# A hybrid encoder layer on one core: two small tiles shift the right-hand pools, and the recurrence's squares are emitted later

## The chip, the cores and the metric

The kernel runs on one core of a Trainium2 chip. The metric is the device time of one execution in microseconds (us), the median of several runs. TensorE multiplies (PE in the rows, PEld for its weight loads), VectorE is DVE, ScalarE is ACT, GpSimd is POOL, and SyncE (SP) issues the DMAs.

## The reference

One layer over a sequence of 1024 positions, width 1024, all in float32:

```
proj = rms_norm(x) @ w_in                       # 512 LRU + 512 gate + 256 + 128 + 32 columns
xc   = depthwise_conv(lru_x)                    # 4 taps
for each direction:                             # forward and backward
    r, i = sigmoid(xc @ w_a + b_a), sigmoid(xc @ w_x + b_x)      # 8 blocks of 64 x 64
    a    = exp(-8 * r * softplus(-lambda))
    h    = scan(a, sqrt(1 - a^2) * (i * xc))    # h_t = a_t h_(t-1) + u_t
y_lru = gelu(lru_g) * (h_forward + h_backward)
y_mla = attention(8 heads, 96 wide keys, 64 wide values)
h = x + concat(rms_norm(y_lru), rms_norm(y_mla)) @ w_o
u = depthwise_conv(rms_norm(h) @ w_up)          # 1024 -> 2 * 2816, 3 taps
out = rms_norm(h + (silu(u[:2816]) * u[2816:]) @ w_down)
```

The group norm of `y_lru` needs, for each position, the sum of the squares of its 512 channels.

## The kernel before, in words

Every product of two float32 matrices is made of three products of a coarse part and a remainder (`split`, lines 60 to 67, and `mm3`, lines 69 to 72), so a 128x128 weight block is loaded for each 128x512 matmul.

**The recurrence.** The 512 channels are four tiles `j` of 128 partitions by 1024 positions. A tile passes through projection (`proj_x`, `proj_g`), convolution (`conv_a`: one ACT instruction, three on DVE; `conv_b`: the split), four gates (`gate`: PE, then a tanh on ACT), decay (`decay_exp`, `square_a`, `decay_tanh` on ACT, `decay_mul` on DVE), a square root on ACT that needs another activation table (`root`), `gated` and `scale_in` (direction 0 on DVE, direction 1 on POOL), the scans on DVE (`scan`), `add_dirs`, two gelu steps and `merge`, which writes `y_lru[:, j]`. `squares(j, t1)` (lines 239 to 247) squares that tile on ACT; for `j` = 0 it writes the sum `qs`, for the others it overwrites the gelu's tile `t1`, and POOL adds that to `qs`. `qs` is read only in the middle of the attention, by `pss` (line 858).

**Who sets the order.** Tiles 0 and 1 stand in the loop over `j`, in a block where only PE keeps the order of the program. The planner of the compiler puts the other engines' instructions in an order of its own: on its own timeline an engine takes the instruction, among those whose inputs are there, that was emitted first. So an instruction can run ahead of many that are emitted before it. After the loop, from `xc3 = conv_a(3)`, a block begins in which PE, ACT, DVE and POOL all keep the order of the program; tiles 2 and 3 lie in it. There `root()` of tile 2 is followed by `gated` and `scale_in` for both directions, `load_kv` (ACT writes the coarse part of `wkv`, POOL its remainder), `scan(0)`, the first gelu step, `scan(1)`, `add_dirs`, and the gates of tile 3. PSUM has three "big" buffers; the projection `psG2` takes the one that the first gate of tile 2 gives back.

**The memory.** SBUF pools are stacked from the left (`cst`, `sm`, `xtp`, `stp`, `wp`, later `ap`, `fw`) and from the right (`keep`, `ctpool`, `xp`, `lp2`, `lp`, `ap2`, `op`, `fp`). A right-hand pool lies below the one opened before it, and its first tile lies lowest. By the kernel's memory map the left-hand matrix tiles begin at multiples of 128 bytes in a partition. The right end is at byte 229,344, which is 32 over a multiple of 64, and since the right-hand matrix tiles are multiples of 512 bytes long, they all begin 32 over a multiple of 64 (96 over a multiple of 128). On the right lie `cT` (latents, and later three of the output projection's weights), `xch` and `gwt` (gate operands), `wn` (latent projection weights), `kt1` (the keys of odd heads), `yl`, `wo67` in `keep`, and `T1`, `T3`, `T4` in `fp`.

**The up projection.** The FFN's first product is done in 22 pairs of column blocks. Each pair is seven products of 12 matmuls (`PRODUCTS`, `prod`, lines 1067 to 1075), in the order 1, 5, 6, 2, 7, 3, 4. The streamed operand of a product is one of seven 512-column forms: `B11`, `B21`, `B22` and `T2` lie on the left (`xtp`), `T1`, `T3` and `T4` on the right (`fp`). The loaded operand `W` is on the left from pair 2 on; for pairs 0 and 1 the first one is a part of `wo345`, on the right.

Of the kernel before, what the change touches and what calls it, by code (L numbers as in the profile page):

```python
# [10 lines left out]
F32 = mybir.dt.float32  # L11
# [6 lines left out]
P = 128  # L18
D = 1024
S = 1024  # L20
NT = S // P
# [9 lines left out]
CH = 2  # L31
NCHUNK = NPAIR // CH
EPS = 1e-6
GK = math.sqrt(2.0 / math.pi)

V_CW, V_CB, V_GB, V_LAM, V_GO, V_FW, V_FB = 0, 16, 20, 36, 44, 52, 184
# [4 lines left out]
def encoder_layer(ctx, tc, x, w_in, wq, wk, wv, gw, wo, wup, wdn, vec, g_mix, g_ffn, g_fin, g_q, g_kv, tab_t, tab_n, out):  # L41
# [6 lines left out]
    def sbpool(name, bufs=1, side="left"):  # L48
        return tc.tile_pool(name=name, bufs=bufs, side=side, reuse_waits="tile")
# [28 lines left out]

    def rsqrt_dve(sq, ss, n, scale, name, bias=-0.5 * EPS):
        def s1(tag):  # L80
            return sm.tile([P, n], F32, tag="%s%d" % (tag, n), bufs=4 if n == 1 else 1, name=name + tag)
        xh, r0, t, t2, r = s1("xh"), s1("r0"), s1("t"), s1("u"), s1("r")
        dve.tensor_scalar(out=xh, in0=ss, scalar1=-0.5 * scale, scalar2=bias, op0=ALU.mult, op1=ALU.add)
        dve.reciprocal(r0, sq)
        dve.tensor_mul(t, r0, r0)
        dve.tensor_mul(t2, t, xh)
        dve.scalar_tensor_tensor(out=r, in0=t2, scalar=1.5, in1=r0, op0=ALU.add, op1=ALU.mult)
        return r
# [37 lines left out]
    eps_c = cst.tile([P, 1], F32, name="eps_c")  # L126
    pool.memset(eps_c, EPS)
    ones = cst.tile([P, 1], F32, name="ones")
# [7 lines left out]

    right = ExitStack()
    keep = right.enter_context(sbpool("keep", side="right"))
    ctp = ExitStack()
    ctpool = ctp.enter_context(sbpool("ctpool", side="right"))  # L140
    cT = ctpool.tile([P, 2, 3, S], F32R, tag="cT", name="cT")
# [73 lines left out]
    def root():  # L215
        act.activation(bc[:, 0:2, :], bc[:, 0:2, :], AF.Sqrt, scale=-0.0625)
# [18 lines left out]
    def gelu_b(t1, p):  # L235
        act.activation(t1, t1, AF.Tanh, scale=GK)
        dve.scalar_tensor_tensor(out=t1, in0=t1, scalar=1.0, in1=p, op0=ALU.add, op1=ALU.mult)

    def squares(j, t1, eng="act"):
        if j == 0:  # L240
            act.activation(qs, y_lru[:, j, :], AF.Square)
            return
        if eng == "act":
            act.activation(t1, y_lru[:, j, :], AF.Square)
        else:
            pool.tensor_tensor(out=t1, in0=y_lru[:, j, :], in1=y_lru[:, j, :], op=ALU.mult)
        pool.tensor_tensor(out=qs, in0=qs, in1=t1, op=ALU.add)
# [4 lines left out]
    if True:  # L252
        with sbpool("xp", side="right") as xp:
# [37 lines left out]
                xT.append([xtp.tile([P, NK, 512], F32R, tag="xT", name=f"xT{hf}{z}") for z in range(2)])  # L291
            lat = keep.tile([P, NT, NAT], F32, tag="keepB", name="lat")
            kp_nat = keep.tile([P, S], F32R, tag="kpT", name="kpT")
            ss_x = xp.tile([P, NT], F32, name="ss_x")
            ss_l = xp.tile([P, NT, 2], F32, name="ss_l")

            def square(i):
# [162 lines left out]
        if True:  # L460
            def conv_a(j):
                p = psx[j]
                xc = lp.tile([P, S], F32, tag=f"xc{j % 2}", name=f"xc{j}")
                cw = lambda t: vv[:, V_CW + 4 * j + t:V_CW + 4 * j + t + 1]
                act.activation(xc, p, AF.Identity, scale=cw(2), bias=vv[:, V_CB + j:V_CB + j + 1])
                dve.scalar_tensor_tensor(out=xc[:, 2:], in0=p[:, :-2], scalar=cw(0), in1=xc[:, 2:], op0=ALU.mult, op1=ALU.add)
                dve.scalar_tensor_tensor(out=xc[:, 1:], in0=p[:, :-1], scalar=cw(1), in1=xc[:, 1:], op0=ALU.mult, op1=ALU.add)
                dve.scalar_tensor_tensor(out=xc[:, :-1], in0=p[:, 1:], scalar=cw(3), in1=xc[:, :-1], op0=ALU.mult, op1=ALU.add)
                return xc

            def conv_b(j, xc):
                xch = lp.tile([P, 2, S], F32R, tag="xch", name=f"xch{j}")
                split(xch[:, 0], xch[:, 1], xc, "dve", "dve")
                return xc, xch

            def conv(j):
                return conv_b(j, conv_a(j))

            def gate(j, d, g):
                gwt, xch = got[f"g{j}"], cv[j][1]  # L480
                psg = bigA(f"psg{j}{d}{g}")
                b = 2 * d + g
                for hf in range(2):
                    mm3(psg[:, ts(hf, 512)], (gwt[:, 0, b, :], gwt[:, 1, b, :]),
                        (xch[:, 0, ts(hf, 512)], xch[:, 1, ts(hf, 512)]), True, True)
                act.activation(bc[:, 2 * g + d, :], psg, AF.Tanh, scale=0.5, bias=gb_h[:, 4 * j + b:4 * j + b + 1])

            def gated(j, d):
                dve.scalar_tensor_tensor(out=bc[:, 2 + d, :], in0=bc[:, 2 + d, :], scalar=1.0, in1=cv[j][0], op0=ALU.add, op1=ALU.mult)

            def a_tiles(j):
                return [lp2.tile([P, S], F32, tag="a", bufs=2, name=f"a{j}{d}") for d in range(2)]

            def a2_tile(j, d):
                return lp.tile([P, S], F32, tag="a2", name=f"a2{j}{d}")

            def t1_tile(j):
                return (lp2 if j % 2 else lp).tile([P, S], F32, tag="gt", name=f"t1{j}")

            def load_gates(j, gst=None):  # L500
                if gst is None:
                    gst = stp.tile([P, 4, P], F32, tag="st", name=f"gst{j}")
                    nc.sync.dma_start(out=gst, in_=gw[:, j])
                g = lp.tile([P, 2, 4, P], F32R, tag="gw", name=f"gwt{j}")
                split(g[:, 0], g[:, 1], gst, "act", "pool")
                return g

            got = {"X1": wx1, "G0": wG0, "g0": load_gates(0, gst0)}

            def load(k, j):  # L510
                got[f"{k}{j}"] = load_gates(j) if k == "g" else load_w((0 if k == "X" else 512) + j * P, f"w{k}{j}", w_in, "act")

            cv = {0: conv(0)}
            proj_x(1, got["X1"])
            cv[1] = conv(1)
            order.close()
            order.enter_context(tc.manual_schedule(engines=ORDER_PE))
            for j in range(2):
                load("X", j + 2)
                aa = a_tiles(j)  # L520
                gate(j, 0, 0)
                gate(j, 1, 0)
                for d in range(2):
                    a2 = a2_tile(j, d)
                    decay_exp(j, d, aa[d])
                    square_a(aa[d], a2)
                    decay_tanh(j, d)
                    decay_mul(d, a2)
                proj_g(j, got[f"G{j}"], 0)
                gate(j, 0, 1)  # L530
                gate(j, 1, 1)
                root()
                for d in range(2):
                    gated(j, d)
                    scale_in(d)
                    scan(d, aa[d])
                add_dirs(dve)
                proj_g(j, got[f"G{j}"], 1)
                t1 = t1_tile(j)
                gelu_a(t1, psG[j])  # L540
                gelu_b(t1, psG[j])
                load("g", j + 1)
                load("G", j + 1)
                proj_x(j + 2, got[f"X{j + 2}"])
                if j == 0:
                    cv[2] = conv(2)
                merge(j, t1, dve)
                squares(j, t1)
            load("G", 3)


# [21 lines left out]
    proj_g(2, got["G2"], 1)  # L573
    decay_mul(1, a2)
    root()
    gated(2, 0)
    gated(2, 1)
    scale_in(0)
# [3 lines left out]
    t1 = t1_tile(2)  # L582
# [522 lines left out]
    fp = fpx.enter_context(sbpool("fp", side="right"))  # L1105
    for f in ("T1", "T3", "T4"):
        B[f] = fp.tile([P, 2, 4, 512], F32R, name=f)
    C11 = {1: fp.tile([P, S], F32, tag="c", bufs=4, name="s1c")[:, lo]}
    for j in range(3):
        tr_sum("T1", j, spare)  # L1110
    copy(C11[1], S1)
    add(C11[1], VL[1], C11[1])
    prod(6, 0, VL[0], False)
# [156 lines left out]
    def norm3_half(i):  # L1270
        junk = fw.tile([P, 512], F32, tag="w3", bufs=2, name=f"jg{i}")
        act.activation(junk, hh[i][:, hi], AF.Square, accum_out=ss_f[:, i:i + 1])
        for k, m in ((0, 1.0), (1, -0.5)):
            dve.tensor_scalar(out=part[:, k, i:i + 1], in0=ss_f[:, i:i + 1], scalar1=m / D, scalar2=m * EPS, op0=ALU.mult, op1=ALU.add)

# [5 lines left out]
    def norm3_dve(i, sq, part_only=False):  # L1281
        r = rsqrt_dve(sq, ss_f[:, i:i + 1], 1, 1.0 / D, f"rf{i}", part[:, 1, i:i + 1] if part_only else -0.5 * EPS)
        for c in ((lo, hi) if i == NT - 1 else (slice(0, D),)):
# [46 lines left out]
    for j in range(1, NPAIR):  # L1330
# [13 lines left out]
        if j > 1:  # L1344
            GL = bank("GL", f"gl{j}")
            C11[j] = GL
            copy(GL, vl)
# [12 lines left out]
        if j > 1:  # L1360
            prod(2, j, C11[j], False)
        VH[e] = bank(f"H{e}", f"vh{j}")
# [7 lines left out]
        else:  # L1370
# [5 lines left out]
            make(3)  # L1376
        cgs[j] = conv_start(j, C11[j])
        prod(3, j, GH, False)
        add(GH, GH, ts_)
        if not last:  # L1380
            prod(4, j, vl, False)
            glu_gate(j, C11[j], GH)
            fetch_raw(j + 2, 1)
# [142 lines left out]
```

## Time and profile before

| what | value |
|---|---|
| median of 3 runs | 1216.63 us (1215.02 to 1218.22) |
| the profiled execution's own time | 1217.72 us |
| its span, first to last instruction | 1215.9 us (1.8 us lie around it) |
| granted TensorE clock, mean | 0.99 of full speed |
| busy share of the span | PE 96%, PEld 80%, DVE 76%, ACT 54%, POOL 20% |
| chain that ended last, by engine | PE 82%, DVE 10%, ACT 3%, DMA 2%, issue 2% |

The chain that ended last is followed back from the last instruction, at each step to what released it. Where it is all PE, only PE's pace counts; where it changes engines, a delay of any link counts. The stages by the trace: norm and latents to 78 us, the recurrence to about 200 us (it overlaps the attention's first tiles), attention to 440 us, output projection and the FFN's first pair to about 615 us, the other pairs of the up projection to about 1005 us, the down projection to the end.

### The profile page before, as it was taken

To read this page: it belongs to the slowest core of one execution; us is meant where nothing else is said; L and a number is where in the kernel's file an instruction comes from. 1 tells how busy PE (TensorE), PEld (TensorE's weight loads), DVE (VectorE), ACT (ScalarE), POOL (GpSimd) and SP (SyncE) were. 2 spreads that over 40 slices of the span, in tenths; PEclk is the share of its full clock that TensorE was granted. 3 is DMA by queue.
4 is the path that set the end of the run, shared out by engine and by line. 5 is a ranking of instruction groups with operands and counts; after the bars stand their busy time and mean duration, and the time that the engine had idled before them with its cause. 6 is when DMAs were issued, how large, how long until landed. Compare 5 with 4: busy or idle time off the path is not lost.

```text
span 1215.9 us, 15339 instructions
## 1 busy us (share of the span) xinstructions
PE 1165.4 (96%) x5668; PEld 970.0 (80%) x5668; DVE 925.7 (76%) x1371; ACT 656.4 (54%) x1055; POOL 241.9 (20%) x138
## 2 busy tenths in 40 slices
PE   5999997999999999998999999999999999999997
PEld 5977775788889888776778888888888888888885
DVE  6787879777777755587687877877787876887866
ACT  5736687776777763343554454444454454443453
POOL 2213435621212433352011110101011000000000
PEclk9999989999999999998999999999999999999999
DMA  5311101000000142230243223332323259753233
GB/s 214 98 42 44 44 18 35 18 1 1 1 1 1 53 157 87 73 118 18 61 130 122 96 78 111 106 113 81 110 95 121 87 173 334 262 183 112 96 113 121
DMA packets 93579, 113.38 MB, mean 93 GB/s; under 512 B 5184, under 2 KB 59840, under 8 KB 93504
## 3 DMA queue, kind: packets, MB, share of 16 engines
q1 hardware_dynamic: 93504, 112.40, 27.9%
q8 instruction: 44, 0.72, 0.3%
q14 instruction: 31, 0.25, 0.1%
HBM read 82.76 MB, written 28.57 MB: 92 GB/s over the span
## 4 chain that ended last, share of the span: by engine, by line
PE 82%; DVE 10%; ACT 3%; DMA 2%; issue 2%; SPq 0%; DVEq 0%; POOL 0%; ACTq 0%
PE vl L1075 19%; PE x L1268 9%; PE y L1268 7%; PE gh L1075 5%; PE gl L1075 4%; PE pt L762 4%; PE p L1075 4%; PE av L773 3%; PE av L772 3%; PE sc L70 2%; PE sc L71 2%; PE sc L72 2%; DVE bc L223 2%; PE pso L71 1%; PE pso L72 1%
## 5 line engine op out<-in xcount | busy, mean ns | idle before, releaser
L1075 PE MATMUL vl<-T,w 128*128 128x512 f32 x792 | 195.7, 396 | 1.8 <-ACT gl L1081 1.5
L1075 PEld LDWEIGHTS vl<-T,w 128*128 128x128 f32 x792 | 148.6, 188 | 37.6 <-ACT gl L1081 1.9
L67 POOL TENSOR_TENSOR w<-rg,w 128x1024 fp32r<-128x1024 f32 x21 | 52.0, 2474 | 363.6 <-ACT w L62 212.3
L62 ACT ACTIVATE ptb<-pt 128x512 fp32r<-128x512 f32 x128 | 70.1, 596 | 57.5 <-PE pt L762 56.3
L748 DVE TENSOR_REDUCE nm<-sc 128x1 f32<-128x1024 f32 x64 | 78.2, 1222 | 29.9 <-PE sc L72 29.6
L67 DVE TENSOR_TENSOR ptb<-pt,ptb 128x512 fp32r<-128x512 f32 x128 | 83.1, 681 | 7.0 <-ACT ptb L62 7.0
L755 ACT ACTIVATE pr<-sc,nm 128x1024 f32<-128x1024 f32 x64 | 71.7, 1121 | 4.2 <-DVE nm L748 4.1
L762 PE MATMUL pt<-ident,pr 128*128 128x128 f32 x512 | 67.7, 274 | 3.8 <-DVE ptb L67 3.8
L762 PEld LDWEIGHTS pt<-ident,pr 128*128 128x128 f32 x512 | 59.2, 140 | 14.7 <-DVE ptb L67 6.0
L1075 PE MATMUL gh<-B,w 128*128 128x512 f32 x264 | 64.4, 393 | 1.4 <-DVE T L67 1.4
L1172 ACT ACTIVATE c<-gh,vv 128x512 f32<-128x512 f32 x22 | 17.1, 778 | 89.1 <-DVE gh L1078 89.1
L772 PE MATMUL av<-ptb,vt 128*128 128x256 f32 x256 | 64.9, 292 | 0.0
L773 PE MATMUL av<-ptb,vt 128*128 128x256 f32 x256 | 62.6, 283 | 0.0
L1075 PE MATMUL p<-T,w 128*128 128x512 f32 x252 | 62.5, 397 | 0.0
L1268 PE MATMUL x<-abS 128*128 128x512 f32 x264 | 60.2, 389 | 0.0
L1268 PE MATMUL y<-abS 128*128 128x512 f32 x264 | 60.2, 389 | 0.0
L1075 PEld LDWEIGHTS gh<-B,w 128*128 128x128 f32 x264 | 49.5, 188 | 13.0 <-DVE T L67 1.6
L1075 PE MATMUL vl<-B,w 128*128 128x512 f32 x240 | 58.4, 392 | 0.0
L1268 PEld LDWEIGHTS x<-abS 128*128 128x128 f32 x264 | 49.6, 188 | 10.3
L1268 PEld LDWEIGHTS y<-abS 128*128 128x128 f32 x264 | 49.6, 188 | 10.3
L1075 PE MATMUL gl<-B,w 128*128 128x512 f32 x240 | 57.7, 389 | 0.0
L1075 PEld LDWEIGHTS p<-T,w 128*128 128x128 f32 x252 | 47.4, 188 | 11.4
(646 smaller groups left out, 2953.8 us busy)
## 6 DMA issues: line engine op xcount, KB each, us to landing
rg<-in_wup SPq DMA_DIRECT2D x22, 512.0 KB, 3.9
rv<-in_wup SPq DMA_DIRECT2D x22, 512.0 KB, 3.7
S<-c SPq DMA_DIRECT2D x44, 256.0 KB, 2.6
wr<-in_wdn SPq DMA_DIRECT2D x44, 256.0 KB, 5.4
stS<-S SPq DMA_DIRECT2D x44, 256.0 KB, 2.9
A<-c SPq DMA_DIRECT2D x33, 256.0 KB, 2.1
stA<-A SPq DMA_DIRECT2D x33, 256.0 KB, 4.0
wost<-in_wo SPq DMA_DIRECT2D x8, 512.0 KB, 3.7
```

The lines of the kernel that those rows point to most:

```text
L62: act.activation(hi, src, AF.Copy)
L67: (dve if lo_on == "dve" else pool).tensor_tensor(out=lo, in0=src, in1=hi.bitcast(F32), op=ALU.subtract)
L70: pe.matmul(ps, l[0], r[0], start=start, stop=False)
L71: pe.matmul(ps, l[0], r[1], start=False, stop=False)
L72: pe.matmul(ps, l[1], r[0], start=False, stop=stop)
L748: dve.reduce_max(nm[t], sc[t], axis=AX, negate=True)
L755: act.activation(pr[t], sc[t], AF.Exp, bias=nm[t], accum_out=rowsum[:, h, i:i + 1])
L762: pe.transpose(pt[:, ts(c, P)], pr[t][:, ts(4 * kh + c, P)], ident)
L772: pe.matmul(av[:, 0:256], lv, ptb[buf][:, 0, c, :], start=(c == 0), stop=False)
L773: pe.matmul(av[:, 0:256], lv, ptb[buf][:, 1, c, :], start=False, stop=(c == NT - 1))
L1075: pe.matmul(ps, w[:, l, ko + k, :], b[:, r, k, :], start=a_, stop=z_, skip_group_check=True)
L1268: pe.matmul(ps, ab[:, 0, l, ts(j, P)], ab[:, 1, r, :], start=a_, stop=z_, skip_group_check=True)
```

## The change

`ss_x` (32 bytes per partition) is allocated first in `keep` instead of in `xp`. So `ctpool` and every right-hand pool opened above it on the stack (`xp`, `lp2`, `lp`, `ap2`, `op`) moves 32 bytes down, while the other tiles of `keep` stay. In `xp` the tiles behind the old place of `ss_x` move with it. In `fp` a tile of 24 floats (96 bytes) that nothing reads is put behind `T1`, `T3` and `T4`, which moves these three 96 bytes down; the `c` tiles behind it stay. And `squares(0)` is emitted behind the `root()` of tile 1 in the loop, `squares(1, t1)` behind the `root()` of tile 2, which is in the block where all engines keep the program's order. No arithmetic changes.

```diff
+PAD = 24
...
     keep = right.enter_context(sbpool("keep", side="right"))
+    ss_x = keep.tile([P, NT], F32, name="ss_x")
     ctp = ExitStack()
...
-            ss_x = xp.tile([P, NT], F32, name="ss_x")
...
                 gate(j, 0, 1)
                 gate(j, 1, 1)
                 root()
+                if j == 1:
+                    squares(0, None)
                 for d in range(2):
...
                 merge(j, t1, dve)
-                squares(j, t1)
             load("G", 3)
...
     decay_mul(1, a2)
     root()
+    squares(1, t1)
     gated(2, 0)
     gated(2, 1)
     scale_in(0)
...
     for f in ("T1", "T3", "T4"):
         B[f] = fp.tile([P, 2, 4, 512], F32R, name=f)
+    fp.tile([P, PAD], F32, name="pad")
```

## Rows read from the trace of the kernel before

**Rows 1.** By stretch: us; busy PE, PEld, DVE, ACT, POOL (count); PE clock, DMA, GB/s
```profile
230.00:330.00 100.00, 99.66 (x651) 88.62 (x652) 77.53 (x123) 70.29 (x135) 24.73 (x18) 1.00 0.00 1
...
600.00:1005.00 405.00, 403.49 (x1744) 327.42 (x1743) 322.05 (x423) 195.29 (x260) 46.23 (x19) 1.00 0.33 108
```

**Rows 2.** Chain that ended last, one pair: start us, us on the chain, what
```profile
617.73 2.72 PE gl L1075 x12
620.45 2.81 PE vl L1075 x12
623.26 2.76 PE gh L1075 x12
626.02 5.57 PE vl L1075 x24
...
637.17 2.72 PE gl L1075 x12
```

**Rows 3.** Instructions of the PSUM tile gl: duration ns min/median/max, first and last start
```profile
L1075 PE MATMUL gl<-B,w x240: 388/389/390, 617.6 to 989.4; 128*128 128x512 f32 x120
L1075 PE MATMUL gl<-B,wo x12: 392/397/478, 554.9 to 557.5; 128*128 128x512 f32 x12
```

**Rows 4.** Busy time of the score matmuls (sc) alone, heads 2 and 3; columns us, PE, PEclk
```profile
263.50:292.80 29.30, 12.57 (x48) 1.00 0.00 1
292.80:323.10 30.30, 12.58 (x48) 1.00 0.01 1
```

**Rows 5.** ACT in order of time: start us, us, line, what, [idle before <-releaser]
```profile
119.30 1.06 ACT L241 ACTIVATE qs<-y_lru 128x1024 f32<-128x1024 f32 x1 [5.68 <-DVE y_lru L229]
...
139.98 1.05 ACT L62 ACTIVATE wG<-wG3s 128x1024 fp32r<-128x1024 f32 x1
...
152.22 1.06 ACT L244 ACTIVATE t<-y_lru 128x1024 f32<-128x1024 f32 x1 [5.69 <-DVE y_lru L229]
153.19 1.19 ACT L465 ACTIVATE xc<-psx,vv 128x1024 f32<-128x1024 f32 x1
154.28 2.11 ACT L486 ACTIVATE bc<-psg,gb_h 128x1024 f32<-128x1024 f32 x2
...
162.64 1.12 ACT L486 ACTIVATE bc<-psg,gb_h 128x1024 f32<-128x1024 f32 x1 [2.90 <-PE psg L72]
...
169.79 1.92 ACT L216 ACTIVATE bc<-bc 128x2048 f32<-128x2048 f32 x1
```

**Rows 6.** DVE in order of time, tile 2's tail and one later scan
```profile
167.99 1.23 DVE L213 SCALAR_TENSOR_TENSOR bc<-a,bc 128x1024 f32<-128x1024 f32 x1 [2.01 <-ACT bc L207]
...
172.52 1.21 DVE L219 TENSOR_TENSOR bc<-bc 128x1024 f32<-128x1024 f32 x1
173.77 4.38 DVE L223 TENSOR_TENSOR_SCAN bc<-a,bc 128x1024 f32<-128x1024 f32 x1
...
179.18 3.32 DVE L223 TENSOR_TENSOR_SCAN bc<-a,bc 128x1024 f32<-128x1024 f32 x1
...
183.67 1.21 DVE L237 SCALAR_TENSOR_TENSOR t<-t,psG 128x1024 f32<-128x1024 f32 x1
...
209.88 2.28 DVE L223 TENSOR_TENSOR_SCAN bc<-a,bc 128x1024 f32<-128x1024 f32 x1
```

**Rows 7.** POOL in order of time, tile 1's addition and tile 2's tail
```profile
153.36 2.35 POOL L247 TENSOR_TENSOR qs<-qs,t 128x1024 f32<-128x1024 f32 x1 [6.83 <-ACT t L244]
...
172.74 3.25 POOL L219 TENSOR_TENSOR bc<-bc 128x1024 f32<-128x1024 f32 x1 [2.37 <-ACT wkv L62]
175.95 4.39 POOL L67 TENSOR_TENSOR wkv<-wkvst,wkv 128x1024 fp32r<-128x1024 f32 x1
```

**Rows 8.** PE in order of time: the last matmul of psx3 and the first of psG2
```profile
149.51 0.39 PE L72 MATMUL psx<-xT,wX 128*128 128x512 f32 x1
...
155.43 0.80 PE L70 MATMUL psG<-xT,wG 128*128 128x512 f32 x1 [2.76 <-ACT bc L486]
```

**Rows 9.** Busy time from 155.43 us on, columns as in Rows 1
```profile
155.43:161.00 5.57, 5.57 (x13) 4.42 (x14) 4.05 (x4) 4.27 (x4) 0.28 (x1) 0.50 0.00 0
```

## The prediction

> **What bounds the kernel now.** I read the stretches first, then the chain inside each. In the attention and in the up projection PE is the bound: it is busy for 99.66 of 100 us and for 403.49 of 405 us, at full clock [rows 1]. A wait removed there on another engine is worth nothing; a faster matmul is worth itself. The chain of the up projection says the same in detail: it is PE alone, and a pair of column blocks takes 637.17 - 617.73 = 19.44 us [rows 2]. The reader is to see that the seven products of a pair, all of 12 matmuls of one shape, do not take the same time: 2.72 us for gl (form `B21`), 2.81 for the one behind it (`T3`), 2.76 for gh (`B22`), 5.57 for the two that follow (`T4`, `B11`), and 637.17 - 626.02 - 5.57 = 5.58 for the last two (`T1`, `T2`). The recurrence (78 to 200 us) is bound by a chain that passes between PE, ACT and DVE; there the timelines by engine count [rows 5 to 8].
>
> **Part one: the 96 bytes in `fp`.** gl, whose two operands both lie on the left, takes 389 ns a matmul with a spread of 2. The same product with the same streamed form took 397 (median) when its weights lay in `wo345`, on the right [rows 3]. So I read the slow products as a matter of place: streamed and loaded operand whose addresses differ by 32 modulo 64 bytes are some 8 ns a matmul slower. `T1`, `T3`, `T4` with left-hand weights are that case. The product behind such a one is slowed too, 2.76 against 2.72, though its own operands are level; gl, which follows a level product, is not. The 96 bytes put the three forms on a multiple of 128, where `B21` is. Then all seven should take 2.72: 7 x 2.72 = 19.04, against 19.44 a saving of 0.40 us a pair. gl with left-hand weights has 240 matmuls [rows 3], so 20 pairs have this form: 8.0 us, all on the chain, since DVE is busy for 322 of these 405 us and ACT for 195 [rows 1], and both fit in 397. Pairs 0 and 1 run among waits for DVE and ACT; I count them at nothing (up to 0.4). Bounds: no gain, if place is not the cause, and 8.4. I take 8.0, since a row with exactly the placement of after exists.
>
> The Trainium skill ("TensorE: Matmul & The Clock Gate", section "Step-by-step: what each phase is for") says that PE has two independent read ports into SBUF and that loading the next weights takes no read bandwidth from the running matmul. By that rule the place of an operand can't matter, this part is worth nothing and the total is that of the second rival below. The two gl rows, 389 and 397 ns, speak against it.
>
> **Part two: the 32 bytes of `ss_x`.** They put `cT`, `wn`, `kt1` and `yl` at 64 modulo 128, so their distance from left-hand partners becomes 64. No row shows that distance. If only the remainder modulo 64 counts, it is as good as level; if not, nothing or a little is lost. The attention shows how little is at stake: the 48 score matmuls of an odd head, whose keys are the shifted `kt1`, are busy 12.58 us, those of an even head with left-hand keys 12.57 [rows 4]. Against this `wo67` in `keep` stays and `yl` moves away from it: 96 matmuls of the output projection become unlevel, 0.8 us at 8 ns, about what 114 others there would gain. The latent projection's 192 matmuls (8 tiles by 24) and the attention's 96 for keys and queries have the rest, 288 x 8 ns = 2.3 us at most, part of it beside waits. I take a gain of 1.0, with ends of -3 and +0.8.
>
> **Part three: `squares(1)` behind the root of tile 2.** The order is now pinned. Front: ACT waited 5.69 us for `merge` before that square, and `conv_a(3)` stood behind it at 153.19 [rows 5], though its input was there with the last matmul of psx3, at 149.51 + 0.39 = 149.90 [rows 8]. It now starts there. The gates behind it follow: the first ends at 149.9 + 1.09 + 1.1 = 152.1, before PE has finished the gates' matmuls at 155.43 - 2.76 = 152.67, so PE doesn't wait for the buffer and 2.76 us of idle time go [rows 5, 8]. After that gap PE ran 13 matmuls in 5.57 us at a granted clock of 0.50 [rows 9], the lower of its levels (1.2 instead of 2.4 GHz); at the 0.227 us each of gl [rows 2] they take 2.95, so another 2.6 us go if the clock stays up. PE is 5.4 us earlier. ACT is free after the second gate at 152.67 + 1.1 = 153.8, then has the 3.36 us of work that stood between 156.38 and 159.74 [rows 5] and reaches the gate of 162.64 at 157.2: 5.4 us earlier as well. `decay_mul` and `scale_in(0)` follow, at 162.6 and 167.1 instead of 167.99 and 172.52 [rows 6].
>
> Tail: ACT gets 1.06 us more between the root and the coarse part of `wkv`. The gelu step and the gates behind are not late by it, since DVE reaches that step only behind the first scan. POOL gets the addition (2.35 us, [rows 7]) ahead of `scale_in(1)` and `wkv`. What it costs depends on one thing that the rows show: a POOL addition or product and a DVE instruction that reads two SBUF tiles exclude each other. A scan takes 2.28 alone but 4.38 and 3.32 here, and POOL's 3.25 and 4.39 are the counterpart [rows 6, 7]: `scale_in(1)` waits until DVE's ends at 173.73, the scan waits until POOL's ends at 175.99, POOL's `wkv` waits for the scan, the next scan for the end of `wkv` at 180.34. In the new order (times of after): `scale_in(0)` 167.1 to 168.3, addition to 170.6, first scan to 172.8, `scale_in(1)` to 175.1. The second scan needs that result, and POOL has `wkv` ready at that moment; POOL goes on without a signal between engines, so I let it be first: `wkv` to 177.3, scan to 179.5, against 182.5 before. So of 5.4 us gained, 2.4 are paid back: 3.0 remain. Ends: 5.2 if the scan is first, 0.7 if the addition gets in ahead of `scale_in(0)` too, which is a matter of 0.1 us (the square ends at 167.2). Behind it hang `add_dirs`, the gelu step of 183.67 that frees PSUM, tile 3's gates (they overwrite `bc`) and, by DVE, the attention's first tiles, so the 3.0 stay. PE now idles longer ahead of that gelu step and may lose its clock once more, but the next 20 matmuls end in a wait anyway.
>
> **Part four: `squares(0)`.** I cost it at nothing, since I don't expect it to move. It was emitted last in its pass and yet ran at 119.30, ahead of tile 2's convolution, which was emitted first: the planner takes what is ready. The split of `wG3` ran at 139.98 [rows 5], though it is emitted behind the square of 152.22. Emitted later, `squares(0)` is still the only thing ready for ACT in that gap. No DMA is issued by the moved steps; SP's loads wait for staging slots that POOL frees, `wkv`'s among them, and these move with POOL.
>
> **Sum.** 8.0 + 1.0 + 3.0 = 12.0. From the profiled execution's own 1217.72 (span 1215.9 and 1.8 around it) that is 1205.7; it stands 1.1 above the median of the runs, 1216.63, from which it is 1204.6. I say 1205.
>
> **Rivals.**
> 1. `squares(0)` moves as well. Then tile 2's convolution doesn't wait for the 5.68 us of 119.30, and as in part three some 4 us more come off: 1201. For it: the same shape of gap. Against it: the two early instructions of [rows 5].
> 2. The place is not the cause of the slow products. Then only parts three and a bit of two remain, 4 us: 1213, within what can be told from no change. For it: the slow forms are also those computed as sums, and no row changes place alone on the streamed side. Against it: the two gl rows.
> 3. POOL's addition gets the port ahead of `scale_in(0)`: 0.7 instead of 3.0, 1207.5.
> 4. Slower: in the attention only PE's order is pinned, and POOL, ACT and DVE are planned anew from a shifted start. From 230 to 440 us some 60 tiles run; one DVE instruction of 1.21 us, like that of 183.67 [rows 6], put ahead of the one PE waits for in every third tile makes PE wait 1.21 x 20 = 24 us: 1205.7 + 24 = 1230. It decides from 12/60 = 0.2 us of new PE wait a tile. Against it: DVE is busy for 77.5 and ACT for 70.3 of 100 us [rows 1], so a changed order has slack.
>
> **How the numbers follow.** Forecast 0.60 (1202.5 to 1207 by itself), rival 1 0.15, rival 3 0.10, rival 2 0.08, rival 4 0.03, the rest is spread. The range 1199 to 1210 takes in rivals 1 and 3 and the bounds of part two, and leaves out the others. A measurement tells 0.3% (3.65 us) from no change; faster is below 1213: forecast, rivals 1 and 3, and most of what is spread, 0.92. Rival 2 is the same, 0.05 with its share that ends below; slower 0.03.
>
> **What would show it.** `p` and `vl<-T` at 389 ns and a pair at 19.04 us: part one; 19.44 refutes it. ACT's convolution of tile 3 near 150, no PE gap near 152 and a clock of 1.00 from there: the front. The second scan of tile 2 behind `wkv` and the gelu step about 3 us early: the tail. The square of tile 0 still ahead of tile 2's convolution: part four. Wrong is the prediction if pairs keep their time, or if PE is idle between 230 and 440.

## The result and the profile after

| | median | runs | profiled execution: own time, span |
|---|---|---|---|
| before | 1217.43 us | 4 (1215.02 to 1219.09) | 1217.72, 1215.9 |
| after | 1204.55 us | 4 (1204.03 to 1206.67) | 1204.52, 1202.7 |

The ratio is 0.9894, with a 95% interval of 0.9875 to 0.9913: 12.9 us faster, where 12.0 was forecast (1205.0 us). What follows asks whether it came out for the forecast reasons, step by step.

The chain that ended last, one pair of the up projection (start us, us on the chain, what); it answers to [rows 2], and lines are left out where the same three come round again:

```profile
612.43 2.72 PE gl L1078 x12
615.15 2.72 PE vl L1078 x12
617.87 2.72 PE gh L1078 x12
620.59 5.44 PE vl L1078 x24
626.03 2.72 PE p L1078 x12
628.75 2.72 PE vl L1078 x12
631.47 2.72 PE gl L1078 x12
```

All seven products take 2.72 us, and the pair takes 631.47 - 612.43 = 19.04 us instead of 19.44. The tile gl, for [rows 3] (duration ns min/median/max, first and last start):

```profile
L1078 PE MATMUL gl<-B,w x240: 389/389/389, 612.3 to 976.5; 128*128 128x512 f32 x120
...
L1078 PE MATMUL gl<-B,wo x12: 393/394/478, 552.6 to 555.2; 128*128 128x512 f32 x12
```

The second line is the first sign against part two. `wo345` now lies 64 bytes off the streamed form, not 96, and its matmuls still take 394 ns, not 389.

By stretch, for [rows 1]: the attention is still all PE, so rival 4 (the attention re-planned to its harm) did not come. DVE and ACT fit beside the shorter pairs.

```profile
230.00:330.00 100.00, 100.00 (x654) 89.14 (x654) 77.23 (x124) 69.76 (x134) 24.91 (x18) 1.00 0.00 1
...
600.00:1005.00 405.00, 403.22 (x1779) 333.58 (x1778) 328.09 (x433) 196.81 (x264) 46.18 (x19) 1.00 0.36 117
```

ACT in order of time, for [rows 5] (start us, us, line, what, idle before and its releaser):

```profile
119.36 1.06 ACT L243 ACTIVATE qs<-y_lru 128x1024 f32<-128x1024 f32 x1 [5.68 <-DVE y_lru L231]
...
149.97 1.21 ACT L466 ACTIVATE xc<-psx,vv 128x1024 f32<-128x1024 f32 x1 [3.38 <-PE psx L73]
...
157.17 1.09 ACT L487 ACTIVATE bc<-psg,gb_h 128x1024 f32<-128x1024 f32 x1
...
164.31 1.92 ACT L218 ACTIVATE bc<-bc 128x2048 f32<-128x2048 f32 x1
166.13 1.04 ACT L246 ACTIVATE t<-y_lru 128x1024 f32<-128x1024 f32 x1
...
174.91 1.12 ACT L487 ACTIVATE bc<-psg,gb_h 128x1024 f32<-128x1024 f32 x1 [3.45 <-POOL bc L221]
```

The square of tile 0 (119.36) has not moved. The convolution of tile 3 starts at 149.97, and what it waits for is now PE's last matmul. The gate that stood at 162.64 starts at 157.17, with no wait (forecast 157.2). The square of tile 1 stands behind the root, at 166.13. The last line is a link that I had named only in passing: the second gate of tile 3 overwrites `bc`, and here it waits 3.45 us for POOL's `scale_in(1)`. PE for [rows 8], and the 5.57 us from its first matmul of psG2, for [rows 9]:

```profile
149.54 0.39 PE L73 MATMUL psx<-xT,wX 128*128 128x512 f32 x1
...
152.58 0.50 PE L71 MATMUL psG<-xT,wG 128*128 128x512 f32 x1
```

```profile
152.58:158.15 5.57, 5.57 (x25) 4.59 (x25) 4.27 (x4) 5.33 (x5) 0.00 (x0) 1.00 0.00 0
```

No wait stands ahead of psG2, the granted clock stays at 1.00 (2.4 GHz), and the same 5.57 us hold 25 matmuls instead of 13. Tile 2's tail on DVE and POOL, for [rows 6] and [rows 7]:

```profile
162.51 1.22 DVE L215 SCALAR_TENSOR_TENSOR bc<-a,bc 128x1024 f32<-128x1024 f32 x1 [2.12 <-ACT bc L209]
...
167.03 1.22 DVE L221 TENSOR_TENSOR bc<-bc 128x1024 f32<-128x1024 f32 x1
168.28 4.39 DVE L225 TENSOR_TENSOR_SCAN bc<-a,bc 128x1024 f32<-128x1024 f32 x1
...
174.91 4.48 DVE L225 TENSOR_TENSOR_SCAN bc<-a,bc 128x1024 f32<-128x1024 f32 x1 [1.12 <-POOL bc L221]
...
180.56 1.22 DVE L239 SCALAR_TENSOR_TENSOR t<-t,psG 128x1024 f32<-128x1024 f32 x1
```

```profile
167.25 3.27 POOL L249 TENSOR_TENSOR qs<-qs,t 128x1024 f32<-128x1024 f32 x1 [2.36 <-ACT t L246]
170.48 4.39 POOL L221 TENSOR_TENSOR bc<-bc 128x1024 f32<-128x1024 f32 x1
174.83 2.40 POOL L68 TENSOR_TENSOR wkv<-wkvst,wkv 128x1024 fp32r<-128x1024 f32 x1
```

POOL's three instructions and DVE's two scans take turns, in the forecast order: `scale_in(0)`, addition, scan, `scale_in(1)`, `wkv`, scan. The second scan ends at 174.91 + 4.48 = 179.39 (forecast 179.5), and the gelu step is 183.67 - 180.56 = 3.11 us early (forecast 3.0).

**Where the time went, matmul by matmul.** PE's order is the same in both kernels, so the start of a matmul, counted from PE's first one, can be set against its own start in before. The names are those of the PSUM tiles in the kernel:

| first matmul of | stage | after - before |
|---|---|---|
| psx3 | ahead of the changed front | -0.17 us |
| psg201 (a later gate of tile 2) | front | -5.47 |
| psk0 | attention's first | -3.31 |
| pt590 | attention's end | -4.05 |
| pshB111 | output projection, behind its third row block of eight | -2.68 |
| vh0 | the FFN's first pair | -5.32 |
| gl3 to gl21 | 18 pairs | -5.91 to -13.11 (0.400 each) |
| x0 | behind the up projection | -13.33 |

The pairs and the recurrence are as forecast. Two terms are not. The output projection loses 1.15 us at one place, where PE waits 1.45 us for DVE's `h`, not 0.34 (first before, then after):

```profile
513.86 1.17 PE L941 MATMUL pshB<-ident,h 128*128 128x128 f32 x8 [0.34 <-DVE h L936]
```

```profile
511.38 1.17 PE L944 MATMUL pshB<-ident,h 128*128 128x128 f32 x8 [1.45 <-DVE h L939]
```

And 2.6 us go between `pshB111` and `vh0`. There the kernel before had lost its clock, by the busy times of that stretch (first before, then after):

```profile
560.00:575.00 15.00, 13.60 (x60) 11.32 (x61) 9.69 (x15) 3.03 (x6) 0.00 (x0) 0.77 0.00 1
```

```profile
560.00:575.00 15.00, 13.70 (x77) 11.43 (x76) 9.81 (x16) 5.22 (x10) 0.00 (x0) 1.00 0.00 1
```

### The profile page after: what moved, and what is told of

It is laid out like the page before. It is cut to its first block, busy times and chain, and to the rows that moved or that the text cites. A ratio compares the mean times of both kernels' runs of the same rounds, so it can differ in the third digit from the quotient of the medians.

```text
span 1202.7 us, 15339 instructions
## 1 busy us (share of the span) xinstructions
PE 1152.7 (96%) x5668; PEld 966.2 (80%) x5668; DVE 926.8 (77%) x1371; ACT 655.6 (55%) x1055; POOL 241.8 (20%) x138
## 4 chain that ended last, share of the span: by engine, by line
PE 75%; DVE 7%; ACT 1%; DMA 1%; issue 1%; DVEq 0%; POOL 0%; ACTq 0%
PE vl L1078 19%; PE x L1272 9%; PE y L1272 7%; PE gh L1078 5%; PE gl L1078 5%; PE pt L765 4%; PE p L1078 4%; PE av L776 3%; PE av L775 3%; PE sc L71 2%; PE sc L73 2%; PE sc L72 2%; PE pso L73 1%; PE pso L72 1%; PE pso L71 1%
## 5 line engine op out<-in xcount | busy, mean ns | idle before, releaser
L1078 PE MATMUL vl<-T,w 128*128 128x512 f32 x792 | 190.8, 390 | 2.3 <-ACT gl L1084 1.8
```

The lines of the kernel that those rows point to most:

```text
L1078: pe.matmul(ps, w[:, l, ko + k, :], b[:, r, k, :], start=a_, stop=z_, skip_group_check=True)
```

## The experiments

Theory: part one is place (operands that don't agree in some low part of their addresses), part three is the moved square. Left open by the result: which part of the address counts (part two assumed the remainder modulo 64), whether the two unforecast terms follow from the change, and whether POOL's addition is what paid 2.4 us back. All ratios are to the kernel before, run beside.

**One: the pad alone.**

```diff
+    fp.tile([P, 24], F32, name="pad")     # before + this
```

> The kernel before plus the 96-byte tile alone; every engine keeps its order of instructions. Theory (place, part one): a pair takes 19.04 us instead of 19.44, 20 pairs, -8.0 us against the kernel before, 1209.4 from its median of 1217.4; and the clock fall that the kernel before shows at 561 to 568 us stays, since nothing ahead of the FFN moves. Rival (place is not the cause, the pairs' gain comes from something that the moved squares bring): pair 19.44, 0 us. Rival (the fall at 561 us is chance): 2.9 us more may go.

1207.50 us, ratio 0.9925 (0.9896 to 0.9955), against 1217.5 for 26 runs of before (1210.92 to 1221.38). Until `pshB111` the first matmul of every PSUM tile starts within 0.15 us of its place in before. Of the 9.62 us that it has won at x0, 9.40 - 2.20 = 7.20 lie in the 18 pairs from gl3 to gl21, 0.400 each:

```profile
653.50 2.72 PE gl L1076 x12
656.22 2.72 PE vl L1076 x12
658.94 2.72 PE gh L1076 x12
661.66 5.44 PE vl L1076 x24
```

So place alone makes part one. The median is 10.0 us lower, 2 us more than the pairs give. In the trace another 1.68 us are won at vh0 already, and from 560 to 575 us the clock is 1.00; whether the 2 us belong to the pad, one trace doesn't tell. My first theory on that fall was wrong: with the same instructions in the same order ahead of it, it is there in one execution (0.77) and gone in another. So the 2.6 us between `pshB111` and `vh0` in the table above can't be put down to the change; nor can the 1.15 us at `pshB111`, for this kernel has a wait of 1.6 us for the same `h` and comes 1.17 us late there. The kernel after itself, profiled a second time (its expectation stands under seven), confirms both: it waits 0.29 us for `h`, and from 560 to 575 us the fall is there, about half as long as in before:

```profile
560.00:575.00 15.00, 13.70 (x70) 11.34 (x70) 10.27 (x17) 5.22 (x10) 0.00 (x0) 0.90 0.01 1
```

**Two: the squares alone.**

```diff
+                if j == 1: squares(0, None)    # behind root(), before + both moves
...
     root()
+    squares(1, t1)
```

> The kernel before with both squares emitted as in the kernel after, and no byte of memory moved. Theory (part three alone): ACT's convolution of tile 3 starts near 150 us, the second scan of tile 2 ends about 3 us early, all that hangs behind is as much early: -3.0 to -3.4 us, pair 19.44. If the square of tile 0 has moved (rival 1) some 4 us more. If the 2.9 us that are gone at 551 to 558 us in the kernel after come from the earlier arrival there, they go here too: -6.

1212.98 us, ratio 0.9971 (0.9956 to 0.9986): 4.5 us. In the trace 3.50 us at psk0 and 3.75 at the attention's end, and no more but for the clock near 561 us (4.89 at x0, the same at gl3 and at gl21). Its second scan of tile 2 runs where that of the kernel after does:

```profile
174.92 4.49 DVE L223 TENSOR_TENSOR_SCAN bc<-a,bc 128x1024 f32<-128x1024 f32 x1 [1.11 <-POOL bc L219]
```

Part three is shown by itself, and it repeats. From psx3, ahead of the front, to the attention's first settled tile (230 us behind PE's first matmul in before), the four executions with the squares in this order (this one, the kernel after twice, run seven) win 3.42 to 3.54 us, and the five with before's order (the pads and run six) lose 0.00 to 0.15. The forecast was some tenths low.

**Three to five: other pads**, to find which part of the address counts.

```diff
-PAD = 24      # 96 bytes
+PAD = 8       # 32 bytes; 56: 224 bytes; 88: 352 bytes
```

> The kernel before plus a tile of 32 bytes instead of 96 in the same place: T1, T3 and T4 come to 64 modulo 128, so 64 from B21 and the left-hand weights. Theory A (my forecast of part two: only the remainder modulo 64 counts): level, pair 19.04 us, -8.0 us. Theory B (the remainder modulo 128 or more counts, as the rows of the kernel after at distance 64 suggest): pair 19.44, 0 us.

> The kernel before plus a tile of 224 bytes instead of 96: T1, T3 and T4 are again at 0 modulo 128, but 128 bytes further down than in the kernel after, so no longer at the same remainder modulo 256 or 512 as the left-hand tiles. Theory B128 (only the remainder modulo 128 counts): pair 19.04 us, -8.0 us. Theory B512 (256 or 512 counts): pair 19.44 us, 0 us.

> The kernel before plus a tile of 352 bytes in fp: T1, T3 and T4 lie 256 bytes further down than in the kernel after. The 96-byte tile gave 0.400 us a pair, the 224-byte one (128 off) 0.13, so a multiple of 128 is not enough. Theory P512 (the operands must agree modulo 512, or more): pair between 19.25 and 19.44 us, -1 to -3.5 us by the pairs. Theory P256: pair 19.04 us, -8.0 us.

One pair in each, first 32 bytes, then 224, then 352:

```profile
657.98 2.76 PE vl L1076 x12
660.75 2.77 PE gh L1076 x12
663.51 5.53 PE vl L1076 x24
```

```profile
658.81 2.79 PE vl L1076 x12
661.60 2.73 PE gh L1076 x12
664.34 5.53 PE vl L1076 x24
```

```profile
660.26 2.72 PE vl L1076 x12
662.98 2.72 PE gh L1076 x12
665.70 5.44 PE vl L1076 x24
```

By the kernel's memory map and the starts of successive matmuls in these traces. The step is the mean time from one matmul's start to the next within a product that streams `T1`, `T3` or `T4` (512 columns, full clock, no wait):

| `T1`, `T3`, `T4` against the left-hand tiles | kernel | mean step | pair | time, ratio |
|---|---|---|---|---|
| 96 bytes off | before | 234 ns | 19.44 us | 1217.5 |
| 64 off | pad 32 | 230 | 19.32 | 1214.29, 0.9976 (0.9957 to 0.9996) |
| 128 off | pad 224 | 233 | 19.30 | 1214.57, 0.9971 (0.9953 to 0.9989) |
| 256 off | pad 352 | 227 | 19.04 | 1206.63, 0.9917 (0.9891 to 0.9943) |
| 0 | pad 96 | 227 | 19.04 | 1207.50, 0.9925 (0.9896 to 0.9955) |

Operands are level when their addresses agree modulo 256, of the distances tried. The rule that I forecast from (modulo 64) falls with the 32 bytes, and the one that I put in its place (modulo 128) with the 224. Modulo 512, the other theory of that run, falls with the 352.

**Six: the 32 bytes of `ss_x` alone** (part two).

```diff
+    ss_x = keep.tile([P, NT], F32, name="ss_x")     # and not in xp
```

> The kernel before with the 32 bytes of ss_x moved alone (part two): same instructions in the same order, right-hand pools at distance 64 instead of 96 (modulo 512) from the left-hand tiles, wo67 as before. My forecast: -1.0 us. Theory (distance 64 is off as 96 is, a little less): the kernel after gained 0.6 us with it in latent projection and attention and lost some of it in the output projection where yl moves away from wo67; -0.6 to +1 us in all, less than this measurement can tell; pair 19.44.

1216.79 us beside 1216.23 of before, ratio 1.0006 (0.9989 to 1.0023): no change that can be told. In the trace it wins 0.43 us from the attention's first settled tile to its end and loses some 0.3 in the output projection, without the wait for `h`, where `yl` moves away from `wo67`: first before, then with the moved `ss_x`:

```profile
L70 PE MATMUL pso01b<-wo,yl x4: 389/389/389, 497.2 to 499.2; 128*128 128x512 f32 x4
```

```profile
L70 PE MATMUL pso01b<-wo,yl x4: 397/399/402, 497.3 to 499.4; 128*128 128x512 f32 x4
```

The first line settles a rival of the reading by distance, that each operand's own address counts. In before both `yl` and its weights lie on the right, 96 over a multiple of 128, and take the same 389 ns as gl with both on the left. What counts is the place of one against the other.

**Seven: all right-hand tiles level.** The right end moves down 96 bytes, made of `ss_x` and `ss_l`; the pad in `fp` goes.

```diff
+    rpad = ctx.enter_context(sbpool("rpad", side="right"))
+    ss_x = rpad.tile([P, NT], F32, name="ss_x")
+    ss_l = rpad.tile([P, NT, 2], F32, name="ss_l")
     right = ExitStack()
...
-        ss_h = op.tile([P, NT], F32, tag="ssh", name="ss_h")
+        ss_h = ss_x
...
-    fp.tile([P, PAD], F32, name="pad")
```

> The kernel after with the right end moved down by 96 bytes instead of its two edits of the memory: ss_x and ss_l (32 + 64 bytes) are put above keep, ss_h is taken into ss_x, the pad in fp goes. All matrix tiles, left and right, agree modulo 512. Theory (level means agreement modulo 512, each off-level matmul of 512 columns costs 4 to 7 ns): pairs stay at 19.04; against the kernel after the attention gains about 2 us (75 matmuls of the queries x 4 ns, 300 of the keys x 4 ns, some 200 ns of the others), the output projection about 1.3 (some 300 x 4.5 ns), the latent projection some tenths: -2.5 to -4 us. Rival (only the up projection is bound by it; the rest hides it): 0 to -0.5.

> The kernel after itself, on the chip and beside the runs of its variants: 1204.5 us. The pairs take 19.04 us again. If the clock fall at 561 us is a matter of chance and not of the change, it may come back here in some execution and cost up to 2.9 us; the kernel before has had 19 of its runs between 1214 and 1219.

1204.37 us (ratio 0.9907, 0.9885 to 0.9930) beside 1205.96 of the kernel after (0.9915, 0.9893 to 0.9937): the times don't tell the two apart. Both keep pairs of 19.04 us. The trace does: the output projection's matmuls are 5 ns faster at the median. First the kernel after in this run, then the level one:

```profile
L72 PE MATMUL pso<-wo,yl x40: 390/394/398, 463.7 to 491.4; 128*128 128x512 f32 x40
```

```profile
L71 PE MATMUL pso<-wo,yl x40: 387/389/389, 463.1 to 490.1; 128*128 128x512 f32 x40
```

From the attention's first settled tile to the end of these matmuls PE wins 3.97 - 2.50 = 1.47 us on before, the kernel after in this run 1.70 - 1.51 = 0.19. So 1.3 us are won on the kernel after, half of the least that I expected. The over-estimate is the attention: 0.71 us against its 0.42, where I had put 2. Its score matmuls take 393 to 396 ns at the median in before and 393 to 395 with all tiles level, not 389, so their pace hangs mostly on something else, which was not found.

**Eight and nine: the two squares.** First `squares(1)` taken out of the tail, then `squares(0)` really moved, each from the kernel after.

```diff
-    squares(1, t1)                     # eight
-        for j in (2, 3):
+        for j in (1, 2, 3):
...
-                root()                 # nine
+                r_ = root()            # root() returns its activation
...
-                    squares(0, None)
+                    with tc.issue_after(getattr(r_, "ins", r_)):
+                        squares(0, None)
```

> The kernel after with squares(1) emitted together with squares(2) and squares(3), early in the attention, so that POOL's addition and ACT's square leave the tail of tile 2. Theory (part three: of 5.4 us won at the front 2.4 are paid back because POOL's addition, scale_in(1) and wkv and DVE's scans exclude each other): without the addition scale_in(1) ends 2.2 us earlier, the second scan follows it, and the attention starts 2.0 to 2.4 us earlier than in the kernel after: -2.2 us. Rival (the tail is bound by ACT's or PE's chain, not by POOL): the second scan moves, but the attention's start stays within 0.5 us.

> The kernel after with squares(0) told to issue behind the root of tile 1, so that it really moves; in the kernel after it still runs at 119.36 us, after 5.68 us in which ACT waits for y_lru, ahead of the convolution of tile 2. Theory (rival 1's price, same shape of gap as at tile 3): the convolution of tile 2 starts up to 5.7 us earlier, PE's gap there and the clock fall at 124 to 128 us shrink: -4 us by the start of the attention. Rival (tile 2's later links, DVE or PE, wait for something else and only the order of waits changes): 0 to -1.

Eight: 1203.88 us, ratio 0.9880 (0.9861 to 0.9899). PE starts the attention 2.31 us earlier than in the kernel after and keeps 1.98 at its end. DVE's scans and POOL's product:

```profile
168.21 4.37 DVE L225 TENSOR_TENSOR_SCAN bc<-a,bc 128x1024 f32<-128x1024 f32 x1
...
173.62 3.32 DVE L225 TENSOR_TENSOR_SCAN bc<-a,bc 128x1024 f32<-128x1024 f32 x1
```

```profile
167.19 3.25 POOL L221 TENSOR_TENSOR bc<-bc 128x1024 f32<-128x1024 f32 x1 [2.36 <-ACT wkv L63]
170.40 4.39 POOL L68 TENSOR_TENSOR wkv<-wkvst,wkv 128x1024 fp32r<-128x1024 f32 x1
```

The second scan ends at 176.94, 2.45 us earlier than in the kernel after: this is the 2.4 that part three let be paid back, and POOL's addition was the payer. The run moves ACT's square (1.04 us) out of the tail too, but it is `scale_in(1)` that moves up, to 167.19, where the addition had stood (167.25).

Nine: 1201.14 us, ratio 0.9852 (0.9836 to 0.9867). The convolution of tile 2 starts 3.8 us earlier, at PE's signal, and the square behind the root:

```profile
116.52 1.21 ACT L466 ACTIVATE xc<-psx,vv 128x1024 f32<-128x1024 f32 x1 [2.76 <-PE psx L73]
...
133.05 1.04 ACT L243 ACTIVATE qs<-y_lru 128x1024 f32<-128x1024 f32 x1
```

PE is 3.98 us ahead of the kernel after in the attention: the price of rival 1, which I had put at 4.

**Ten: all of it together** (seven, eight and nine).

> All matrix tiles in agreement modulo 256 as in the run with the level right end, squares(0) pinned behind the root of tile 1, and squares(1) with 2 and 3 in the attention. If the gains add (level right end -1.6 by its median, squares(0) -4, squares(1) -2.2 against the kernel after): about 1197 us. If both squares' gaps are one and the same slack, 1200.

1197.11 us (1196.67 to 1198.52), ratio 0.9821 (0.9805 to 0.9836), the fastest. At the attention's first matmul (psk0) PE is 11.29 us ahead of before, and the parts are 3.31 (the kernel after), 2.31 (eight) and 8.82 - 3.31 = 5.51 (nine), 11.13 in all: the gains add, as far as single executions tell (with before's order alone psk0 came 1.26 us early to 1.05 late), and the median is the forecast 1197.

## Why the prediction was right, and where it was not

- **Part one, 8.0 us: right, cause and size.** The pad alone gives 19.04 us a pair. The Trainium skill ("TensorE: Matmul & The Clock Gate", section "Step-by-step: what each phase is for") says that loading the next weights takes no read bandwidth from the running matmul. If that were all, place could not matter, and it does: moving three tiles, and nothing else, took 7 ns (234 to 227) from each of their matmuls. Rival 2 is out. The rule behind it, "differ by 32 modulo 64", was wrong all the same (part two). It did no harm here, because 96 bytes make the three tiles level by the measured rule too.
- **Part two, 1.0 us: the step that failed.** I wrote "If only the remainder modulo 64 counts, it is as good as level", and took a gain. Level is modulo 256 by the pads; 64 off costs 230 ns by pad 32 against 227. What I measured is +0.6 us with an interval of 0.9989 to 1.0023, and in the trace a gain of about 0.1. The size was within my ends of -3 and +0.8, the reason was wrong. The equal score matmuls (12.58 and 12.57 us), on which I leaned, say little on place: they stay above 389 ns where all tiles are level. With all tiles level the attention wins 0.71 us.
- **Part three, 3.0 us: right, a little low.** Front and tail came as worked out, 5.47 us won at psg201, and 3.1 us (from psx3 to psk0) to 3.5 (to the settled attention) left. Rival 3 (the addition ahead of `scale_in(0)`) did not come: `scale_in(0)` ran at 167.03 and the addition got through behind it. That order hung on 0.1 us, and I don't count it as foreseen.
- **Part four, 0: right.** The planner still put `squares(0)` at 119.36. Pinned, it moves, and is worth the 4 us of rival 1.
- **The sum.** 8.0 + 1.0 + 3.0 = 12.0 against 12.9 by the medians and 13.2 by the two profiled executions. In the latter: 8.0 in the pairs, 4.05 up to the attention's end (3.3 at its first matmul, the rest mostly `ss_x`), 2.85 from the clock fall near 561 us, -1.15 from the wait for `h` and some -0.4 in the rest of the output projection. The fall and the wait come and go without the change, as the pad alone and the second profile of the kernel after show, so a forecast from one execution carries them as an error of 2 to 3 us. I did not see the fall near 561 us in the profile of before, and had no term for it. That the total came within 1 us is therefore in part luck: these two terms alone make 1.7 us of the difference of the two profiled executions, and no part of the forecast held them. Run one by one, the parts gained 10.0, -0.6 and 4.5 us by the medians.

What stays open: why the remainder counts (which access delays which) no run here tells; I know only the steps by distance. What keeps the score matmuls above 389 ns was not found, nor what decides whether the clock falls near 561 us.

## What to carry to other kernels

Where two rows of one form differ by a few ns, set the operands' addresses side by side and vary the distance in several steps before trusting a rule: a pad of 32 bytes looked as good as one of 96 on paper and gave 0.12 us a pair, not 0.40. An instruction that waits for a late result on an engine with a fixed order belongs behind the next thing that the engine can do, but only an explicit order moves it when a planner takes whatever is ready. And before a moved instruction is counted as free, look at what else its helpers (here POOL's addition) exclude.

## What the runs showed of the hardware

- In the up projection a streamed and a loaded operand whose addresses differ by 64, 96 or 128 bytes modulo 256 cost 230 to 234 ns a step of 512 columns, those that agree modulo 256 cost 227 (table of the pads). It is the distance that counts: two operands that both lie 96 over a multiple of 128 take 389 ns a matmul, like two level ones (run six).
- The product behind an unlevel one starts slow even though its own operands are level (2.77 us for gh behind `T3` with the 32-byte pad, 2.73 with 224, 2.72 where all are level). In the trace of before its first eight matmuls or so have slow steps, and the last four have 227 ns.
- The granted clock can fall in one execution and not in another at the same place of the same instruction stream (0.77 and 1.00 from 560 to 575 us in before and with the pad alone, 1.00 and 0.90 in two executions of the kernel after).
